# Where the last two column sums of the sample path keep their PSUM banks

## The chip, the cores and the metric

The kernel runs on one core of a Trainium2 chip. Its time is the device time of one execution in microseconds (us). The runs before the change gave 1930.2, 1940.83 and 1928.2 us, with a median of 1930.2 us. Less is better.

## The reference

One layer of a decoder is computed for two groups of tokens that share all weights: a prompt of 1024 rows, and a sample of 8 rows, one new token for each of 8 sequences with 8192 cached positions. All arrays are fp32 with a model width of 1024.

```python
q, k, v, logf, u, z = mixer_inputs(rmsnorm(x, g_mix), w_in, ...)     # 8 heads of 64, and a gating branch
x = x + merge_heads(attention, gating, g_att_out, g_sgu_out, w_o)    # sample: attention over a paged cache
x = x + cross_attend(rmsnorm(x, g_cross), mk, mv, w_cq, w_co)        # 4 heads into 256 memory tokens
h = rmsnorm(x, g_ffn) @ w_up                                         # 1024 -> 2 x 2816
hc = conv_b + sum_i conv_w[i] * shifted(h, i)                        # causal, width 3
x = x + (silu(gate) * val) @ w_down                                  # 2816 -> 1024
y = rmsnorm(x, g_final)
```

Both groups go through all of it, and return `y` together with the new keys, values and convolution rows. The part that matters here is the end: the feed-forward step and the final norm, for the sample's 8 rows and for the second half (512 rows) of the prompt.

## The kernel before

**Two streams.** `prompt()` and `sample()` are generators. The loop at lines 1763 to 1777 draws the prompt's steps and puts steps of the sample between them, at a pace that `PACE` gives. This fixes the order in which the instructions are traced. The order in which each engine then gets them is settled when the program is built: a planner (line 1848) plays the traced program through in a time of its own, gives each tile a buffer, and writes one list for each engine. Each engine works through its list in order; an instruction that waits holds up all that stand behind it on its engine.

**Dense products of the prompt.** Each fp32 product is made of three matmuls on a high and a low part (`gemm3`, lines 242 to 248). `wload` (226) loads a weight tile of 512 KB over SyncE's queue into the ring `wr` (4 buffers, line 223), and `split` makes the high part on ScalarE (209, ring `wh`, 5 buffers) and the low part on VectorE (210, ring `wl`, 4 buffers). In `ffn` (1159) the columns go in four groups of 6, 6, 5 and 5 pairs. A group runs its up products (24 matmuls each, written in the profile as `u,wh` and `u,wl`), evacuated by ScalarE (1192, 1193) and VectorE (1194, 1195, 1197), then its eight down products (15 matmuls each in the last group, `wh,u` and `wl,u`).

**PSUM.** There are eight banks. `BA()` takes from a ring of four, `BB()` from a ring of two (`MB` is 0), and `BK()` (123) hands out in turn two of `BA` and one of `BB`. All dense products take their bank from `BK`. Two more banks, `ms` and `dv`, have one buffer each (129, 132). They serve the decode of the sample and, once that is done, the rest of the sample path.

**The end of the sample path** (`sample_rest`, 1479). Weights come over GpSimd's queue in loads of 1 MB into the ring `kv` (4 buffers). In the up step, each of 22 loads feeds eight products with 256 columns into `dv` (1614); after two loads ScalarE copies the bank (1624) and four small products fold it into `ms` (1629). The activation follows (1634 to 1643). In the down step, each of 11 loads (1648) feeds four products with 512 columns (1653): two into a bank `dv`, two into a bank `ms`, in column groups of 32 partitions that are still to be added up. The profile lists each of these fp32 products as two rows. At the end ScalarE copies each bank to SBUF (1664), one product with a 0/1 matrix adds the four column groups (1666), and VectorE adds the result to the residual (1513). Up to the change this last product takes its bank from `BK()`: the first sum takes one of `bb`, the second one of `ba`. The final norm of the sample and its two stores (1668 to 1674) end this path.

**The end of the prompt path.** After the last down products come the residual add (932), the squares (204), the scale (1242) and the store (1243) of each block of rows.

Of the kernel before, what the change touches and what calls it, by code (L numbers as in the profile page):

```python
# [11 lines left out]
AF = mybir.ActivationFunctionType  # L12
# [66 lines left out]
def build(nc, tc, ctx, a, phases=None):  # L79
# [13 lines left out]
    def nm(s):  # L93
        cnt[0] += 1
        return f"{s}_{cnt[0]}"
# [13 lines left out]
    def KV():  # L109
        return dpool.tile([P, 2048], F32, tag="kv", bufs=NKV, name=nm("kv"))  # L110
# [4 lines left out]
    def BA():  # L115
        return psum.tile([P, 512], F32, tag="ba", bufs=4, name=nm("ba"))

    def BB():
        return psum.tile([P, 512], F32, tag="bb", bufs=2 + MB, name=nm("bb"))
# [3 lines left out]
    def BK():  # L123
        turn_[0] += 1
        return BB() if turn_[0] % BR == BR - 1 else BA()
# [3 lines left out]
    def MS():  # L129
        return BB() if MB else psum.tile([P, 512], F32, tag="ms", bufs=1, name=nm("ms"))  # L130

    def DV():
        return psum.tile([P, 512], F32, tag="dv", bufs=1, name=nm("dv"))

    def D2(n=512, dt=F32):
        return dpool.tile([P, 512], dt, tag="d2", bufs=5, name=nm("d2"))[:, :n]
# [5 lines left out]
    mmul = nc.tensor.matmul  # L142
# [12 lines left out]
    selS = cp[:, C_SELS : C_SELS + 8]  # L155
# [1323 lines left out]
    def sample_rest(xs):  # L1479
# [32 lines left out]
        def add(n, ps):  # L1512
            nc.vector.tensor_tensor(xs[n], ps, xs[n], op=ALU.add)
# [65 lines left out]
        for n in range(2):  # L1579
            ps = MS()  # L1580
# [22 lines left out]
        for f4 in range(11):  # L1603
            ps = DV()
            for q in range(2):
# [6 lines left out]
                for k in range(8):  # L1612
# [5 lines left out]
                        start=(k < 4),  # L1618
                        stop=(k >= 4),
# [3 lines left out]
            t = D2()  # L1623
# [21 lines left out]
        ys = [DV(), MS()]  # L1645
        for f2 in range(0, NF, 2):
            raw = KV().rearrange("p (f d) -> p f d", f=2)
            nc.gpsimd.dma_start(raw, a["w_down"][f2 * P : (f2 + 2) * P, :].rearrange("(f p) d -> p f d", p=P))
            for q in range(2):
                f = f2 + q  # L1650
                j = f % 4
                for n in range(2):
                    mmul(
                        ys[n][32 * j : 32 * j + 32, :],
                        g[:, f * 8 : f * 8 + 32],
                        raw[:, q, n * 512 : (n + 1) * 512],
                        start=(f < 4),
                        stop=(f >= NF - 4),
                        tile_position=(0, 32 * j),
                    )  # L1660
            yield 1
        for n in range(2):
            t = D2()
            nc.scalar.activation(t, ys[n], AF.Copy)
            ps = BK()
            mmul(ps[:8, :], selS, t, start=True, stop=True)
            add(n, ps[:8, :])
        r = rms8(xs)
        for n in range(2):
# [85 lines left out]
    def sample():  # L1755
        yield from decode()
        phase[1] = "rest"
        yield from sample_rest(pair("dec"))
# [111 lines left out]
```

## Time and profile before

| | us |
|---|---|
| runs | 1928.2, 1930.2, 1940.83; median 1930.2 |
| the profiled execution: its own time | 1933.38 |
| its span (first to last record) | 1931.6 |
| TensorE busy (PE) in the span | 1821.0 (94%) |
| VectorE, ScalarE, GpSimd busy | 1403.6, 760.8, 475.3 |
| bytes moved in the span | 517.07 MB |

A row of the timeline gives the start in us, the time to the end of the last instruction merged into it, engine, line, operation, `out<-in` and the count; in brackets stands the idle time of the engine before it and what ended it. PE is the matmul side of TensorE, PEld its weight loads. Ends of matmuls are modelled, so the rate is read from the distance of the starts. A table by windows gives for each stretch the busy time of each engine with its count of instructions, then the granted TensorE clock (1.00 is full) and the share of time in which the DMA engines were busy.

### The profile page before, as it was taken

To read this page: it belongs to the slowest core of one execution; us is meant where nothing else is said; L and a number is where in the kernel's file an instruction comes from. 1 tells how busy PE (TensorE), PEld (TensorE's weight loads), DVE (VectorE), ACT (ScalarE), POOL (GpSimd) and SP (SyncE) were. 2 spreads that over 40 slices of the span, in tenths; PEclk is the share of its full clock that TensorE was granted. 3 is DMA by queue.
4 is the path that set the end of the run, shared out by engine and by line. 5 is a ranking of instruction groups with operands and counts; after the bars stand their busy time and mean duration, and the time that the engine had idled before them with its cause. 6 is when DMAs were issued, how large, how long until landed. Compare 5 with 4: busy or idle time off the path is not lost.

```text
span 1931.6 us, 24224 instructions
## 1 busy us (share of the span) xinstructions
PE 1821.0 (94%) x9255; PEld 1300.7 (67%) x9255; DVE 1403.6 (73%) x1662; ACT 760.8 (39%) x1435; POOL 475.3 (25%) x429
## 2 busy tenths in 40 slices
PE   8999989778898999999999999998999998999798
PEld 5987667555676667777767776675665776667456
DVE  4888668777687786989989899888764459553134
ACT  5332356566632535333333233335353333332122
POOL 1322232322123232223331323343312012101200
PEclk9999999899999999999999999998999998999899
DMA  8877988744496875869787889888769467767841
GB/s 322 288 240 274 332 316 294 255 154 144 158 358 242 317 291 196 304 258 347 283 310 289 312 294 362 322 325 308 282 259 344 163 205 252 290 174 290 332 156 65
DMA packets 156372, 517.07 MB, mean 268 GB/s; under 512 B 20168, under 2 KB 41928, under 8 KB 123488
## 3 DMA queue, kind: packets, MB, share of 16 engines
q0 software_dynamic: 56400, 339.04, 47.1%
q1 hardware_dynamic: 92944, 163.89, 24.4%
q10 hardware_dynamic: 6912, 12.59, 1.7%
q8 instruction: 73, 1.20, 0.2%
q14 instruction: 43, 0.35, 0.1%
HBM read 493.63 MB, written 21.84 MB: 267 GB/s over the span
## 4 chain that ended last, share of the span: by engine, by line
PE 64%; DVE 7%; DMA 4%; ACT 3%; issue 2%; POOL 0%; DVEq 0%; POOLq 0%; ACTq 0%; SPq 0%
PE ba L246 9%; PE ba L247 9%; PE ba L248 9%; PE bb L246 5%; PE bb L247 5%; PE bb L248 5%; PE dv L1371 5%; DMA kv<-cache_k,kidx 2%; DVE kv L1312 1%; DMA kv<-w_down 1%; DVE s L1316 1%; PE ba L973 1%; PE ba L975 1%; PE ba L974 1%; PE dv L1614 1%
## 5 line engine op out<-in xcount | busy, mean ns | idle before, releaser
L209 ACT ACTIVATE wh<-wr 128x1024 fp32r<-128x1024 f32 (+2 forms) x220 | 228.8, 1044 | 474.9 <-PE ba L247 147.1
L210 DVE TENSOR_TENSOR wl<-wr,wh 128x1024 fp32r<-128x1024 f32 (+2 forms) x220 | 262.4, 1200 | 146.0 <-PE ba L248 60.6
L1312 DVE TENSOR_TENSOR kv<-kv,d 128x2048 f32<-128x2048 f32 (+1 forms) x139 | 292.4, 2114 | 33.9 <-DMA kv<-cache_k,kidx 31.9
L1306 POOL DMA_INDIRECT kv<-cache_k,kidx x128 | 179.6, 1403 | 556.0 <-DVE s L1316 251.0
L1316 DVE TENSOR_REDUCE s<-kv 128x32 f32<-128x2048 f32 (+1 forms) x139 | 292.1, 2106 | 0.6
L1365 POOL DMA_INDIRECT kv<-cache_v,kidx x128 | 176.2, 1376 | 419.1 <-PE dv L1371 162.4
L246 PE MATMUL ba<-wh,u 128*128 128x512 f32 (+1 forms) x591 | 224.2, 381 | 0.0
L247 PE MATMUL ba<-wl,u 128*128 128x512 f32 (+1 forms) x591 | 223.8, 379 | 0.0
L248 PE MATMUL ba<-wh,u 128*128 128x512 f32 (+1 forms) x591 | 220.8, 378 | 0.5 <-DVE u L210 0.5
L246 PE MATMUL ba<-u,wh 128*128 128x512 f32 (+2 forms) x528 | 206.7, 392 | 1.3 <-DVE u L213 1.2
L247 PE MATMUL ba<-u,wh 128*128 128x512 f32 (+2 forms) x528 | 207.3, 393 | 0.0
L248 PE MATMUL ba<-u,wl 128*128 128x512 f32 (+2 forms) x528 | 206.3, 391 | 0.0
L1371 PE MATMUL dv<-kv,s 128*32 128x512 f32 x1024 | 135.8, 609 | 4.8 <-DMA kv<-cache_v,kidx 4.8
L246 PE MATMUL bb<-u,wh 128*128 128x512 f32 (+2 forms) x336 | 134.9, 401 | 2.2 <-DVE u L213 2.2
L247 PE MATMUL bb<-u,wh 128*128 128x512 f32 (+2 forms) x336 | 133.3, 397 | 2.5 <-DVE u L213 2.5
L248 PE MATMUL bb<-u,wl 128*128 128x512 f32 (+2 forms) x336 | 132.6, 395 | 0.0
L246 PEld LDWEIGHTS ba<-wh,u 128*128 128x128 f32 x591 | 111.3, 188 | 30.1 <-issue 7.1
L248 PEld LDWEIGHTS ba<-wh,u 128*128 128x128 f32 x591 | 110.8, 188 | 26.7 <-issue 4.6
L247 PEld LDWEIGHTS ba<-wl,u 128*128 128x128 f32 x591 | 111.3, 188 | 22.7 <-issue 2.1
L246 PEld LDWEIGHTS ba<-u,wh 128*128 128x128 f32 x528 | 100.3, 190 | 32.9 <-issue 8.0
L247 PEld LDWEIGHTS ba<-u,wh 128*128 128x128 f32 x528 | 100.5, 190 | 31.9 <-issue 11.3
L248 PEld LDWEIGHTS ba<-u,wl 128*128 128x128 f32 x528 | 100.4, 190 | 28.6 <-issue 8.9
(419 smaller groups left out, 3124.1 us busy)
## 6 DMA issues: line engine op xcount, KB each, us to landing
wr<-w_up SPq DMA_DIRECT2D x88, 512.0 KB
kv<-w_up POOLq DMA_DIRECT2D x22, 1024.0 KB
wr<-w_down SPq DMA_DIRECT2D x40, 512.0 KB
kv<-w_down POOLq DMA_DIRECT2D x11, 1024.0 KB
wr<-w_in SPq DMA_DIRECT2D x16, 512.0 KB
wr<-w_o SPq DMA_DIRECT2D x16, 512.0 KB
wr<-w_cq SPq DMA_DIRECT2D x16, 512.0 KB
wr<-w_co SPq DMA_DIRECT2D x16, 512.0 KB
```

The source lines that it names most:

```text
L209: nc.scalar.activation(h, src, AF.Copy)
L210: nc.vector.tensor_tensor(l, src, h.bitcast(F32), op=ALU.subtract)
L246: mmul(out, sh, mh, start=(i == 0), stop=False)
L247: mmul(out, sh, ml, start=False, stop=False)
L248: mmul(out, sl, mh, start=False, stop=(i == n - 1))
L973: mmul(pss[i], mh[k][:, tb], wh, start=(k == korder[0]), stop=False)
L974: mmul(pss[i], mh[k][:, tb], wl, start=False, stop=False)
L1306: nc.gpsimd.indirect_dma_start(kv, None, a["cache_k"], off(kidx[:, b, ch : ch + 1]))
L1312: nc.vector.tensor_tensor(kvv[:, i : i + m, :], kvv[:, i : i + m, :], qb.unsqueeze(1).broadcast_to((P, m, 512)), op=ALU.mult)
L1316: nc.vector.tensor_reduce(s[:, ch * 4 + i : ch * 4 + i + m, :].rearrange("p k h -> p (k h)"), kvv[:, i : i + m, :].rearrange("p k (h d) -> ...
L1365: nc.gpsimd.indirect_dma_start(kv, None, a["cache_v"], off(kidx[:, b, ch : ch + 1]))
L1371: mmul(dv[32 * j : 32 * j + 32, :], s[:, ch * 4 : ch * 4 + 4, :].rearrange("p k h -> p (k h)"), kvv[:, j, :], start=(ch == 0), stop=(ch == ...
```

## The change

At the end of `sample_rest` the two copies now stand ahead of the two products, and the two products take their banks from `DV()` and `MS()` in place of `BK()`.

```diff
+        ts = [D2(), D2()]
         for n in range(2):
-            t = D2()
-            nc.scalar.activation(t, ys[n], AF.Copy)
-            ps = BK()
-            mmul(ps[:8, :], selS, t, start=True, stop=True)
+            nc.scalar.activation(ts[n], ys[n], AF.Copy)
+        for n in range(2):
+            ps = (DV, MS)[n]()
+            mmul(ps[:8, :], selS, ts[n], start=True, stop=True)
             add(n, ps[:8, :])
```

`ys[0]` holds the one `dv` bank and `ys[1]` the one `ms` bank until its copy has read it. `BK()` counts its calls, so that with two calls fewer each later dense product takes the ring that the product two turns before it would have had; from 15 later products, ten had `ba` and five `bb`, and the pattern of two to one goes on.

## The prediction

> **What bounds the kernel now.** The first view is the page: the span, and the rows of TensorE and of its granted clock over 40 slices of 48.3 us each.
>
> ```profile
> span 1931.6 us, 24224 instructions
> PE   8999989778898999999999999998999998999798
> PEclk9999999899999999999999999998999998999899
> ```
>
> TensorE is busy in nearly every slice, and the slices of the second half that fall below 9 with a lower clock are few. The 38th (1787 to 1835 us) is one. The table by windows is the second view, with cuts set where the dense products of the prompt stop and start again.
>
> ```profile
> core 0: us, PE busy (x) PEld busy (x) DVE busy (x) ACT busy (x) POOL busy (x), PEclk, DMA share, GB/s
> 1700.00:1804.00 104.00, 104.00 (x677) 72.92 (x676) 43.16 (x66) 30.87 (x51) 14.12 (x20) 1.00 0.76 254
> 1804.86:1855.81 50.95, 35.70 (x219) 12.68 (x218) 4.21 (x8) 5.99 (x11) 9.39 (x14) 0.80 0.82 320
> 1855.81:1923.90 68.09, 68.05 (x291) 54.08 (x290) 37.06 (x60) 23.24 (x47) 2.19 (x4) 1.00 0.16 56
> ```
>
> Up to 1804 us TensorE has no gap. Then come 51 us in which it works on the sample alone, with holes and at a clock of 0.80, while VectorE and ScalarE rest. Behind them stand 68 us of dense products with hardly any sample work and an idle DMA (0.16). So two kinds of work that overlapped before run one after the other here. The timeline of TensorE shows the seams:
>
> ```profile
> 1804.67 0.40 PE L248 MATMUL ba<-u,wl 128*128 128x512 f32 x1
> ...
> 1854.86 1.02 PE L1666 MATMUL bb<-d,cp 128*8 128x512 f32 x2 [0.76 <-ACT d L1664]
> 1855.81 0.50 PE L246 MATMUL bb<-u,wh 128*128 128x512 f32 x1
> ...
> 1859.98 1.02 PE L1666 MATMUL ba<-d,cp 128*8 128x512 f32 x2
> 1860.93 0.50 PE L246 MATMUL ba<-u,wh 128*128 128x512 f32 x1
> ```
>
> The first dense matmul after the hole is into `bb`, directly behind the sum in `bb`. The first into `ba` follows directly behind the sum in `ba`. By the code the next two calls of `BK()` after the sums give `ba`, then `bb`: the `ba` product is the earlier one, and yet it starts 5.1 us later, in the middle of the `bb` product. What the two products share with the sums is only the ring. I read this as: a ring gives out its buffers in traced order, so no product traced after a sum gets a bank before that sum has one, and the sum gets it only when the sample's last load has been worked off. The other thing that could hold these products is their weights. VectorE's rows of line 210 for `wl` speak against it (the last before the hole and the next one):
>
> ```profile
> 1805.11 1.23 DVE L210 TENSOR_TENSOR wl<-wr,wh 128x1024 fp32r<-128x1024 f32 x1 [3.36 <-PE ba L248]
> ...
> 1866.75 1.23 DVE L210 TENSOR_TENSOR wl<-wr,wh 128x1024 fp32r<-128x1024 f32 x1 [1.42 <-PE ba L248]
> ```
>
> No split for the up products lies between 1805.11 and 1866.75. From 1855.81 to 1866.75 there is time for some 43 dense matmuls beside the second sum, nearly two products of 24, so the weights of at least two were ready by 1806.3.
>
> **The change part by part.** *Removed:* two draws on the rings. The dense products then no longer stand behind the sample's tail, and TensorE may take them in the hole. The hole runs from the next dense start that was due (a dense matmul every 0.23 us, 68.09 / 291 from the table; 1804.67 + 0.23 = 1804.90) to 1855.81: 50.9 us. In it the sample's own work has to be done all the same, at full clock. Its prices come from the stretches where it lay between dense products:
>
> ```profile
> 1792.59 1.07 PE L1614 MATMUL dv<-kv,xsT 128*32 128x256 f32 x16
> 1793.60 1.06 PE L1629 MATMUL ms<-cp,d 128*128 128x8 f32 x8
> 1794.58 1.07 PE L1614 MATMUL dv<-kv,xsT 128*32 128x256 f32 x16
> 1795.58 0.50 PE L247 MATMUL ba<-u,wh 128*128 128x512 f32 x1
> ...
> 1842.32 1.06 PE L1653 MATMUL dv<-kv,d 128*32 128x512 f32 x4 [0.64 <-DMA kv<-w_down]
> 1843.20 1.03 PE L1653 MATMUL ms<-kv,d 128*32 128x512 f32 x4
> ...
> 1828.64 1.32 PE L1653 MATMUL dv<-kv,d 128*32 128x512 f32 x6
> 1829.99 1.26 PE L1653 MATMUL ms<-kv,d 128*32 128x512 f32 x6
> ```
>
> - Up step: a group of 16 rows takes 1.0 us (1794.58 to 1795.58). The timeline has six such groups after 1804.90, so 6.0 us.
> - Folds: 0.98 us for 8 rows (1793.60 to 1794.58), four of them: 3.9 us.
> - Down step, 11 loads: four rows take 0.88 us (1842.32 to 1843.20), so a load alone takes 1.76. Where two loads lie ready they overlap: from 1828.64 to the last start of the x6 row (1829.99 + 1.26 - 0.60 = 1830.65) 16 rows take about 2.2, or 1.1 for each load. The first four loads were issued before 1821, ahead of the activation, and will lie ready together: 4 x 1.1 = 4.4. The other seven I count alone: 7 x 1.76 = 12.3. Together 16.7, between 11 x 1.0 = 11.0 (the row of line 1568 below) and 11 x 1.76 = 19.4.
> - The first sum: 0.95 (1854.86 to 1855.81). The second costs the same in both.
> - Breaking into a dense run:
>
> ```profile
> 1672.06 1.06 PE L1568 MATMUL dv<-kv,d 128*32 128x512 f32 x8
> 1673.06 0.50 PE L246 MATMUL ba<-u,wh 128*128 128x512 f32 x1
> ...
> 1675.34 1.06 PE L1568 MATMUL dv<-kv,d 128*32 128x512 f32 x8
> ```
>
> The period is 3.28 us: 1.00 for the eight rows, nine dense matmuls at 0.23 (2.08), and 0.20 for the switch. I count 12 visits (four in the up step, the burst of four loads as one, seven single loads): 2.4 us; at most 15, at least 10.
>
> The sum: 50.9 - (6.0 + 3.9 + 16.7 + 0.95 + 2.4) = 50.9 - 29.95 = **21 us gained**. With the dear ends (19.4, 15 visits) it is 17.6, with the cheap ones (11.0, 10 visits) 27.0.
>
> *What hides the sample's waits now.* A load that comes late was paid in full in the hole; now there is dense work to take. Whether the list has it in the right places is the planner's doing. The waits of TensorE from 1364 to 1804 us, the whole stretch in which this path ran between dense products, are five rows, of 9.4 us in all, and none names a DMA; the longest is
>
> ```profile
> PE bb L246 <- DVE t L1197: 7.0, 1, 7.0
> ```
>
> So I take nothing for new waits. The upper bound is what the weight loads cost the down step in the hole, from the waits of 1800 to 1860:
>
> ```profile
> PEld dv L1653 <- DMA kv<-w_down: 13.6, 7, 4.3
> ```
>
> That is 13.6 us if every one of them stayed. DMA has the room: 50.95 us at 320 GB/s and 68.09 at 56 are 20.1 MB. Spread over some 98 us that is 205 GB/s, under the 254 of 1700 to 1804, where TensorE had no gap.
>
> *Added:* the sum now waits until the bank it writes has been copied. It waits for that copy already, as its operand: the quoted 0.76 before line 1666 is a wait on line 1664. Behind it on TensorE's list dense products can stand, which lose at most that 0.76 once. *Moved:* the second copy stands ahead of the first sum in the trace, but in the list the two copies are neighbours already, so nothing. The instruction and DMA counts stay. *Shifted:* the products after the sums change rings by two turns; the mix stays two to one, and from 1855.81 to 1923.90 TensorE was busy 68.05 of 68.09 us, so evacuation had room: nothing, and below 1 us either way.
>
> *The end.* These rows carry it:
>
> ```profile
> 1854.21 0.60 ACT L1664 ACTIVATE d<-dv 128x512 f32<-128x512 f32 x1 [29.43 <-PE ms L1653]
> ...
> 1864.69 0.99 SPq L1674 DMA_DIRECT2D o_ys<-dec  x2
> ...
> 1923.46 0.40 PE L248 MATMUL ba<-wh,u 128*128 128x512 f32 x1
> ```
>
> The last dense row starts at 1923.46 and the span ends 8.1 us later, with the last norm and store of the prompt. This tail keeps its length. What comes late next: the sample's down step was worked off at 1854 and its stores were issued at 1864.69; the dense products would end about 1923.9 - 21 = 1903. The sample's tail may slip by some 35 us before it is the end.
>
> *The clock.* A table of short windows shows it in the hole:
>
> ```profile
> 1815.00:1820.00 5.00, 3.74 (x32) 0.51 1.03 415
> ```
>
> The columns are TensorE's busy time, the clock (0.51), DMA share and GB/s; the dense stretches have 1.00. This is why I priced by rows at full clock. [...]
>
> **The rivals.**
> 1. *The list has the sample's steps too early.* The planner expects a load sooner than it lands, and TensorE stands at a down step with dense products behind it. For it: the loads of the hole did come late. Against: no DMA wait in 440 us of the same pattern. Price: between half and all of the 13.6, so 7 to 14 less gain: 1916 to 1923.
> 2. *The change does not do what it says.* If something other than the ring held the dense products, the hole stays: 1930, within 3 us. Against: the seams at 1855.81 and 1860.93, and the weights that were ready.
> 3. *Slower: the sample's tail becomes the end.* If dense products, once free, run ahead of the sample throughout, all 67 us of them are done by 1804.9 + 67.1 = 1872; the sample's stretch of 50.9 us then follows alone, to 1923; then copies, sums, norm and stores, 10.5 us as from 1854.21 to 1864.69, and about 2 to land: 1936 instead of 1931.6, about 1934 by the median. It decides once the tail slips by more than the 35 us. Against: at 1792.59 and at 1672.06 the sample's steps break into the middle of a dense product, so they go first when ready.
>
> **How the numbers follow.** The profiled execution's own time is 1933.38, 1.8 above its span and 3.2 above the median of the runs. 1933.38 - 21 = 1912.4, and by the median 1930.2 - 21 = 1909. The forecast's own bounds are 1903 (27.0) and 1913 (17.6); I give it 0.73, the first rival 0.15, the second 0.08, the third 0.04. The range goes from 1903 to 1923 and takes in the first rival; outside are the other two, 0.12, and the edges. A measurement of this kernel tells about 1% from no change, which is 19.3 us. Four fifths of the forecast lie beyond it: 0.73 x 0.8 = 0.58, rounded to 0.60 faster by over 1%. The rest of the forecast, the first two rivals and most of the third make 0.37 within 1%, and 0.03 is left for slower by over 1%.
>
> **What would show it.** The profile after should have dense rows (lines 246 to 248) between the rows of line 1653, no stretch of over 5 us without them before the last of the down products, a granted clock of 1.00 from 1800 on, the two sums back to back in `dv` and `ms`, and the last dense row at about 1903. Everything up to about 1804 us should stand as before. DMA waits before line 1653 with dense rows right behind them would show rival 1; an unchanged hole rival 2; a last store on line 1674 rival 3. The prediction fails by size if the down step costs other than 1.1 to 1.76 us for a load between dense rows.

## The result and the profile after

The changed kernel takes 1909.36 us (median of 1904.94, 1906.85, 1911.87 and 1913.18), the kernel before 1930.97 us (median of 1928.2, 1930.2, 1931.75 and 1940.83). By the medians that is 21.6 us less; the ratio on record is 0.9878, with a 95% interval of 0.9854 to 0.9903. The forecast was 1909. The profiled execution took 1913.18 us. In this kernel the sums stand on line 1667 and the sample's stores on line 1675; lines up to 1660 keep their numbers.

First the page of the kernel after: its span, and TensorE and its clock over 40 slices.

```profile
span 1911.4 us, 24216 instructions
...
PE   8999999778898999999999999998999999899998
...
PEclk9999999989998999999999999998999999899999
```

Before, the 38th slice was a 7 with a clock of 8. Now no slice from the 31st on is below 8 in either row. The table by windows, cut at the same places as before but for the last cut, which is near the end of the dense work, shows what took its place.

```profile
core 0: us, PE busy (x) PEld busy (x) DVE busy (x) ACT busy (x) POOL busy (x), PEclk, DMA share, GB/s
1700.00:1804.00 104.00, 104.00 (x662) 73.19 (x661) 44.11 (x68) 31.52 (x52) 13.41 (x19) 1.00 0.73 252
1804.86:1855.81 50.95, 50.95 (x331) 35.89 (x325) 22.78 (x35) 18.78 (x32) 7.84 (x11) 1.00 0.76 276
1855.81:1903.00 47.19, 47.19 (x195) 28.03 (x192) 18.43 (x31) 11.53 (x28) 3.79 (x6) 1.00 0.34 128
```

TensorE is busy in all of the 50.95 us (35.70 before), at full clock (0.80 before), and VectorE and ScalarE work beside it (22.78 and 18.78 us, 4.21 and 5.99 before). DMA, which stood at 0.82 and then at 0.16, is spread (0.76 and 0.34). The timeline of TensorE has the seams:

```profile
1802.70 1.07 PE L1614 MATMUL dv<-kv,xsT 128*32 128x256 f32 x16
1803.70 1.06 PE L1629 MATMUL ms<-cp,d 128*128 128x8 f32 x8
1804.69 1.07 PE L1614 MATMUL dv<-kv,xsT 128*32 128x256 f32 x16
1805.69 0.50 PE L248 MATMUL ba<-u,wl 128*128 128x512 f32 x1
...
1843.95 1.08 PE L1653 MATMUL dv<-kv,d 128*32 128x512 f32 x8
...
1846.55 1.08 PE L1653 MATMUL ms<-kv,d 128*32 128x512 f32 x8
1847.55 0.50 PE L247 MATMUL ba<-u,wh 128*128 128x512 f32 x1
...
1854.75 0.40 PE L248 MATMUL bb<-u,wl 128*128 128x512 f32 x1
1855.08 1.06 PE L1653 MATMUL dv<-kv,d 128*32 128x512 f32 x4
1855.96 1.03 PE L1653 MATMUL ms<-kv,d 128*32 128x512 f32 x4
1856.92 0.50 PE L246 MATMUL bb<-u,wh 128*128 128x512 f32 x1
...
1886.80 1.02 PE L1667 MATMUL dv<-d,cp 128*8 128x512 f32 x2
1887.66 1.02 PE L1667 MATMUL ms<-d,cp 128*8 128x512 f32 x2
...
1903.80 0.40 PE L248 MATMUL ba<-wh,u 128*128 128x512 f32 x1
```

The sample's rows (1614, 1629, 1653) now stand between dense rows (246 to 248); the longest stretch without a dense row is the burst of four loads, 3.6 us from 1843.95. The sums stand back to back in `dv` and `ms`, and the dense work goes on for 16 us behind them.

To measure the gain in one execution I set both at the same step, the second group of an up-step visit just ahead of the hole. In the timeline of before it is this row:

```profile
1802.86 1.07 PE L1614 MATMUL dv<-kv,xsT 128*32 128x256 f32 x16
```

It answers to 1804.69 after, so this execution was 1.83 us later up to there. From that row to the last dense row it is 1923.46 - 1802.86 = 120.60 us before and 1903.80 - 1804.69 = 99.11 after: 21.5 us. From there to the end of the span it is 8.1 and 7.6, so 22.0 in all. Together with the 1.83 this is the 20.2 between the two spans. So 21.5 of the 22.0 us were gained in the window that the prediction named, and the other 0.5 in the tail behind it.

### The profile page after: what moved, and what is told of

It is laid out like the page before. It is cut to its first block, busy times and chain, and to the rows that moved or that the text cites. A ratio compares the mean times of both kernels' runs of the same rounds, so it can differ in the third digit from the quotient of the medians.

```text
span 1911.4 us, 24216 instructions
## 1 busy us (share of the span) xinstructions
PE 1816.1 (95%) x9255; PEld 1296.3 (68%) x9255; DVE 1404.6 (73%) x1662; ACT 761.7 (40%) x1435; POOL 480.6 (25%) x429
## 4 chain that ended last, share of the span: by engine, by line
PE 66%; DVE 8%; ACT 3%; DMA 3%; issue 2%; POOL 0%; SPq 0%; DVEq 0%; POOLq 0%; ACTq 0%
PE ba L247 9%; PE ba L246 9%; PE ba L248 9%; PE bb L246 6%; PE bb L247 5%; PE bb L248 5%; PE dv L1371 5%; DMA kv<-cache_k,kidx 2%; DVE kv L1312 1%; DVE s L1316 1%; PE dv L1614 1%; PE ba L973 1%; PE ba L975 1%; PE ba L974 1%; PE bb L772 1%
## 5 line engine op out<-in xcount | busy, mean ns | idle before, releaser
L1312 DVE TENSOR_TENSOR kv<-kv,d 128x2048 f32<-128x2048 f32 (+1 forms) x139 | 292.3, 2113 | 28.2 <-DMA kv<-cache_k,kidx 26.9
L1365 POOL DMA_INDIRECT kv<-cache_v,kidx x128 | 181.3, 1416 | 424.2 <-PE dv L1371 169.6
L246 PE MATMUL ba<-wh,u 128*128 128x512 f32 (+1 forms) x596 | 226.9, 382 | 0.0
L248 PE MATMUL ba<-wh,u 128*128 128x512 f32 (+1 forms) x596 | 223.4, 380 | 1.0 <-DVE u L210 1.0
L246 PE MATMUL ba<-u,wh 128*128 128x512 f32 (+2 forms) x520 | 203.0, 391 | 1.3 <-DVE u L213 1.2
L247 PE MATMUL ba<-u,wh 128*128 128x512 f32 (+2 forms) x520 | 203.8, 392 | 0.0
L246 PE MATMUL bb<-u,wh 128*128 128x512 f32 (+2 forms) x344 | 138.2, 402 | 1.8 <-DVE u L213 1.8
L247 PE MATMUL bb<-u,wh 128*128 128x512 f32 (+2 forms) x344 | 136.5, 397 | 2.5 <-DVE u L213 2.5
```

The source lines that it names most:

```text
L246: mmul(out, sh, mh, start=(i == 0), stop=False)
L247: mmul(out, sh, ml, start=False, stop=False)
L248: mmul(out, sl, mh, start=False, stop=(i == n - 1))
L1312: nc.vector.tensor_tensor(kvv[:, i : i + m, :], kvv[:, i : i + m, :], qb.unsqueeze(1).broadcast_to((P, m, 512)), op=ALU.mult)
L1365: nc.gpsimd.indirect_dma_start(kv, None, a["cache_v"], off(kidx[:, b, ch : ch + 1]))
```

## The experiments

**The theory.** A ring gives out its banks in traced order. The two sums draw on the rings and can't be given a bank until the sample's last load has been worked off, so every dense product traced behind them waits for that moment. The rivals: the order of copy and sum, the turns of the rings, or merely sharing a ring, whenever it is drawn on.

**One part alone, and the other (`x1_order`, `x2_banks`).** The change has two parts. The first run has only the copies ahead of the sums, the second only the banks:

```diff
 # x1_order: both copies first, as in the change, and then
             ps = BK()
 # x2_banks: copy, sum, copy, sum as before, but
-            ps = BK()
+            ps = (DV, MS)[n]()
```

> Only the order of the change: both copies stand ahead of both sums, and the sums keep their banks from the prompt's rings. If the rings held the dense products back, the hole of 51 us stays and the time is that of before, 1930 within 4. If the reordering of the copies made the gain, it is 1909.

> Only the banks of the change: each copy is followed by its sum as before, but the sums go to dv and ms. If the rings were the cause, the whole gain is here: 1909 within 4, no stretch without dense rows over 5 us. If the order was the cause: 1930.

The order alone gave 1927.56 us beside 1928.86 for before in the same runs, a ratio of 0.9998 (0.9987 to 1.001). Its trace still has the hole: no dense row starts between 1801.08 and 1849.24. That is a hole of 47.9 us, 3.0 shorter than in the trace of before, with the loads coming at 339 GB/s in place of 320; the medians show no gain from it. The banks alone gave 1907.39, a ratio of 0.9883 (0.9865 to 0.9901), and from the common step to the last dense row their trace takes 99.1 us, as after the change. No gain that can be measured is left for the order.

**The turns of the rings (`x5_shift`).** With two draws fewer, later products change rings. This run has the whole change and puts the turns back:

```diff
             add(n, ps[:8, :])
+        turn_[0] += 2
```

> The change, with the turn counter moved on by two, so that all dense products behind the sums take the rings that they took before the change. If the shift of turns is worth nothing, as I counted it: 1909 within 4. If a part of the gain came from another mix of ba and bb at the end: slower than the change by that part, up to 1930.

1906.76 us, ratio 0.9893 (0.9877 to 0.9909), which is the change's own gain. From the common step to the last dense row its trace, too, takes 99.1 us. The shift of turns is worth nothing that can be measured.

**Sharing a ring, or the place in the trace (`x6_late`).** Here the sums draw on the rings as before, but the sample's last step is traced behind all steps of the prompt:

```diff
+        while not done[0]:
+            yield 1
         for n in range(2):
             t = D2()
             nc.scalar.activation(t, ys[n], AF.Copy)
             ps = BK()
```

(`done[0]` is set behind the loop that draws the prompt's steps.)

> The sums keep their banks from the prompt's rings, with everything else of the kernel before, but the sample's last step is traced only when the whole prompt has been traced. If a ring gives out its buffers in traced order, no dense product stands behind the sums any more and the hole is gone, though the banks are still shared: 1909, and up to 5 more because the sums now get a bank only behind the last dense products, and the sample's norm and stores (some 8 us) may end last. If it is the sharing of the banks as such that costs: 1930.

1911.66 us, ratio 0.9909 (0.9892 to 0.9925): 17.2 us less than before, although the banks are shared. The timeline of TensorE ends like this:

```profile
1904.37 0.40 PE L248 MATMUL ba<-wh,u 128*128 128x512 f32 x1
1904.70 1.03 PE L1668 MATMUL bb<-d,cp 128*8 128x512 f32 x2
1905.56 1.02 PE L1668 MATMUL ba<-d,cp 128*8 128x512 f32 x2
```

And the stores in SyncE's queue:

```profile
1900.11 10.32 SPq L1243 DMA_DIRECT2D o_y<-u  x5
1911.79 0.96 SPq L1676 DMA_DIRECT2D o_ys<-dec  x2
```

The hole is gone, and dense work ends at 1904.37, about as after the change (1903.80). The sums are held until then, and so the sample's stores are now the last thing, 3.0 us ahead of the end of the span (1914.8). This is the third rival of the prediction in a mild form: the sample's tail as the end, for some 3 to 4 us. So it isn't the sharing that made the hole; it is that the sums stood ahead of dense products in the traced order.

**Half the change (`x3_ba`, `x4_bb`).** The first sum has its own bank, the second one still draws on one of the rings. By the theory, products of the other ring run on and those of this ring stop:

```diff
-            ps = (DV, MS)[n]()
+            ps = (DV, BA)[n]()      # x3_ba; (DV, BB) in x4_bb
```

> The change, but the second sum takes a bank of the ba ring; the first one goes to dv. If each ring gives out its buffers in traced order, only the products that take a ba bank are held. The seven up products behind the sums take bb, ba, ba, bb, ba, ba, bb. The first and the fourth can run; the seventh can't, because its low part finds no buffer in wl while the second and third keep theirs. So 48 dense matmuls, 11 us, move into the hole: 1919 within 4. If one sum in either ring holds back all dense products: 1930. If what counts is that one ring is free: 1909.

> The change, but the second sum takes a bank of the bb ring; the first one goes to dv. By traced order in each ring the products in bb are held (first, fourth, seventh), and those in ba can run: second, third, fifth and sixth, 96 dense matmuls or 22 us, about all that the hole has room for, with their results left in the four ba banks. So near the change: 1910 within 5. If one sum in either ring holds back all dense products: 1930.

`x3_ba` took 1925.3 us beside 1932.72 for before, ratio 0.9968 (0.9956 to 0.9981), and `x4_bb` 1922.0, ratio 0.9941 (0.9924 to 0.9958). Both counts of products that ran ahead came true, two whole ones in `bb` and four in `ba`, and both times came out too high. The timeline of TensorE in `x3_ba`:

```profile
1799.58 1.07 PE L1614 MATMUL dv<-kv,xsT 128*32 128x256 f32 x16
...
1822.25 0.50 PE L246 MATMUL bb<-u,wh 128*128 128x512 f32 x1
1822.58 0.40 PE L247 MATMUL bb<-u,wh 128*128 128x512 f32 x1
...
1855.71 1.02 PE L1667 MATMUL dv<-d,cp 128*8 128x512 f32 x2 [0.75 <-ACT d L1664]
1856.57 1.02 PE L1667 MATMUL ba<-d,cp 128*8 128x512 f32 x2
1857.52 0.50 PE L246 MATMUL ba<-u,wh 128*128 128x512 f32 x1
```

The `bb` products stop at 1822.58, and the next dense row, into `ba`, starts directly behind the sum in `ba`. The two rows at 1822.25 and 1822.58 belong to the third `bb` product: they need only the high part of its weights, and it stops ahead of line 248, where it needs the low part, for which the expectation had found no buffer in `wl`. Measured from the row at 1799.58 (1802.86 before), the first sum starts 56.13 us later, and 52.00 before: it slipped by 4.1 us. With these two, 50 dense matmuls, 50 x 0.23 = 11.5 us of dense work, were moved ahead; less the slip that is 7.4, and 7.4 was measured. In `x4_bb`:

```profile
1805.51 1.07 PE L1614 MATMUL dv<-kv,xsT 128*32 128x256 f32 x16
...
1840.00 0.40 PE L248 MATMUL ba<-u,wl 128*128 128x512 f32 x1
...
1870.28 1.02 PE L1667 MATMUL dv<-d,cp 128*8 128x512 f32 x2 [0.75 <-ACT d L1664]
1871.14 1.02 PE L1667 MATMUL bb<-d,cp 128*8 128x512 f32 x2
1872.10 0.50 PE L246 MATMUL bb<-u,wh 128*128 128x512 f32 x1
```

Four products, 96 x 0.23 = 22.1 us, ran ahead and were used up at 1840.00. The rest of the sample's tail then lay bare for 30 us; the sum starts 64.77 us after the row at 1805.51, a slip of 12.8. 22.1 - 12.8 = 9.3, and 10.7 was measured by the medians. In the traces, from the common step to the last dense row (1912.44 and 1916.37), the two gains are 7.7 and 9.7. My expectations had counted only the dense work moved ahead. As long as products stand behind the sums, each microsecond by which that work delays the sums is lost again. In the change no dense product waits for the sums, and the slip is free as long as the sample's tail has room.

**The length of the hole (`x7_before_nodown`, `x8_after_nodown`, `x9_before_nodown_paced`).** The last test takes nine of the eleven loads of the down step away, with their products, from both kernels (the sample's output is then incomplete):

```diff
-        for f2 in range(0, NF, 2):
+        for f2 in range(0, 4, 2):
```

> The kernel before without 9 of the 11 loads of the sample's down step and their products (the sample's output leaves these terms out). In the hole the down step lasts as long as its loads and products: from 1825 to 1854 it would shrink to 3.4 us. So the time falls by about 25: 1906 within 4. If the hole were set by something other than the sample's tail: 1930.

> The changed kernel without the same 9 of 11 loads of the sample's down step (the sample's output leaves these terms out). If the down step costs nothing but its time on TensorE between dense products, the time falls by 2 loads of a burst at 0.86 and 7 single ones at 1.94 (1.84 and the switch, from the timeline of the change): 15 us, to 1894 within 4. If its loads still set the end, it falls by more, up to the 25 of the kernel before.

After the change this gave 1896.11 us, 36.6 below the 1932.72 of before, of which the change is 21.6: nine loads are worth about 15.0 us. By the rows of after, two loads of the burst and seven single ones, each with its switch, are 2 x 0.86 + 7 x 2.04 = 16.0 (my expectation had 1.94 for a single one). In the traces the stretch from the common step to the last dense row takes 99.11 us after the change and 83.05 here (1805.15 to 1888.20), 16.1 less. So the down step costs between dense products what its rows say.

Without the change it gave 1917.01, ratio 0.9924 (0.9908 to 0.9941), where I had expected 1906. The timeline of TensorE shows why:

```profile
1763.29 0.40 PE L247 MATMUL bb<-u,wh 128*128 128x512 f32 x1
...
1810.67 1.88 PE L1666 MATMUL ba<-d,cp 128*8 128x512 f32 x4 [0.77 <-ACT d L1664]
1812.48 0.50 PE L246 MATMUL ba<-wh,u 128*128 128x512 f32 x1
...
1821.61 0.39 PE L248 MATMUL bb<-u,wl 128*128 128x512 f32 x1
```

The dense products stop at 1763.29, more than 40 us earlier than before, in the middle of the sample's up step. Each load is also a step in the loop that mixes the two streams. With nine steps fewer the sums are traced earlier, ahead of more dense products, and the hole begins earlier and is 49 us long all the same. With nine loads gone from both kernels, the change is still worth 1917.01 - 1896.11 = 20.9 us.

These rows show one thing more. The turns fall otherwise here, and both sums draw on `ba` (the row of four). Even so the first `bb` product stops behind its first two matmuls and goes on with line 248 only at 1821.61. By the code its low part needs a buffer of `wl`, and the held `ba` products keep that ring's four (three for a down product, one for an up product); no run takes this apart. Held work can so hold a ring on which no sum draws, as with the third `bb` product of `x3_ba`.

If the reading of the steps holds, keeping nine empty steps must bring the start of the hole back:

```diff
-        for f2 in range(0, NF, 2):
+        for f2 in range(0, 4, 2):
             ...
             yield 1
+        for _ in range(9):
+            yield 1
```

> The kernel before without nine of the eleven loads of the down step, as in the run on the kernel before that left out the same nine, but the nine steps of the two streams' loop that belonged to these loads are kept, empty, so that the two sums are traced between the same dense products as in the kernel before. The sample's output is incomplete. Theory (a product waits for the sums if it is traced behind them, so the place in the traced order sets where the block begins, and the sample's tail sets where it ends): dense products stop at about 1805 us as before, not at 1763, and start again once two loads, copy and first sum are done, at about 1831; 25 us below the kernel before, 1905 +- 4 by its median of 1930. Rival (the place in the trace is not what begins the block; with the loads gone the planner itself puts the products off): dense products stop at about 1763 again, and the time is that of the run without these steps, 1917.

1905.78 us, ratio 0.9873 (0.9833 to 0.9914). The timeline of TensorE:

```profile
1800.56 0.40 PE L248 MATMUL ba<-u,wl 128*128 128x512 f32 x1
...
1802.88 1.07 PE L1614 MATMUL dv<-kv,xsT 128*32 128x256 f32 x16
1804.96 1.07 PE L1614 MATMUL dv<-kv,xsT 128*32 128x256 f32 x16 [1.01 <-DMA kv<-w_up]
...
1807.85 1.07 PE L1614 MATMUL dv<-kv,xsT 128*32 128x256 f32 x16 [0.83 <-DMA kv<-w_up]
1809.64 1.88 PE L1629 MATMUL ms<-cp,d 128*128 128x8 f32 x8 [0.72 <-ACT d L1624]
...
1825.37 1.88 PE L1668 MATMUL bb<-d,cp 128*8 128x512 f32 x2 [0.76 <-ACT d L1666]
1827.18 0.80 PE L246 MATMUL bb<-u,wh 128*128 128x512 f32 x1
1827.77 0.63 PE L247 MATMUL bb<-u,wh 128*128 128x512 f32 x1
...
1829.90 0.39 PE L246 MATMUL bb<-u,wh 128*128 128x512 f32 x1
```

The last dense row ahead of the hole starts at 1800.56 and the next behind the first sum, at 1827.18: the hole begins where it began before (four dense matmuls behind the same group of the up step), not at 1763, and at 26.4 us it is shorter by the missing loads. Where the sums are traced sets the hole's beginning, and when the sample's tail is done sets its end.

## Why the prediction was right

- **What bounds the kernel: right.** The products were held by the rings' traced order. `x2_banks` shows that the banks are the cause, `x6_late` that it is the order of draws and not the sharing, `x3_ba`, `x4_bb` and `x9_before_nodown_paced` that hole and sums go together.
- **The hole of 50.9 us and what still has to run in it: right, with two terms off that cancel.** I read each price as in the prediction, from the first row of a visit to the next dense start, with the switch (0.20) apart. A group of the up step still takes 1.00 us (1804.69 to 1805.69) and a fold 0.99 (1803.70 to 1804.69), or 0.81 for the last one, which stands alone. There are 12 visits, as counted. Four loads side by side were put at 4.4 us and took 3.6 (1843.95 to 1847.55). A load alone was put at 1.76 and took 1.84 (1855.08 to 1856.92), so seven are 12.9. The first sum was 0.86 and not 0.95. The corrected sum is 6.0 + 3.8 + 3.6 + 12.9 + 0.86 + 2.4 = 29.6, and 50.9 - 29.6 = 21.3; from the common step to the last dense row the trace gives 21.5. Both kinds of load lie outside the 1.1 to 1.76 us that the prediction named as its sign (0.90 and 1.84); only the average of the eleven, 1.50, lies inside. That the two errors cancel is luck, and so is a median within 0.4 us of the forecast, where the runs of the changed kernel lie 8.2 us apart.
- **No new waits: right.** From 1800 us to the end the table of waits has no row for the matmul side of TensorE, and no row that names a DMA. The first rival (steps listed before their loads land) did not come about.
- **The added wait of the sums: nothing, as put.** The copies were done long ahead of the sums. ScalarE's rows:

```profile
1881.63 0.60 ACT L1664 ACTIVATE d<-dv 128x512 f32<-128x512 f32 x1 [10.83 <-PE ms L1653]
1882.13 0.59 ACT L1664 ACTIVATE d<-ms 128x512 f32<-128x512 f32 x1
```

The sums start only at 1886.80, behind dense products that the list had put ahead of them. That order costs the sums 4 us and TensorE nothing.
- **The end: right, with more room than I gave it.** SyncE's rows:

```profile
1892.76 0.95 SPq L1675 DMA_DIRECT2D o_ys<-dec  x2
1899.29 9.52 SPq L1243 DMA_DIRECT2D o_y<-u  x5
```

From the common step to the sample's stores it is now 88.07 us, before 61.83: they slipped by 26.2. With the 3.0 us that `x6_late` shows from those stores to the end of the span, they could be 1911.4 - 3.0 - 1892.76 = 15.6 later still. That makes about 42 us of room where I had put 35. Neither decided anything, but the slip is as large as the gain itself, and `x6_late` shows the room used up.
- **The change does what it says**, so the second rival fell with the hole itself.

The gain of 1.1% by the medians (1.2% by the ratio) is only just beyond the 1%, or 19.3 us, that the prediction put as the least that can be told from no change; by the ratio's interval it is 18.7 to 28.2 us.

## What to carry to other kernels

Where a ring gives out its buffers in traced order, as in this kernel, it holds back everything that is traced behind a late taker, however long ago its buffers came free. So give a late, small consumer a buffer that nothing early shares, or trace it behind the products that must not wait; then check that its own tail still has room before the end. When a stall is only moved in part, subtract the delay that the moved work gives to the event that ends the stall. And where the streams are mixed by counting steps, taking work out also moves everything that is traced after it: keep the steps when you take out the work.

## What the runs showed of the hardware

Two things that the sum had only roughly or not at all. First, column groups side by side: by the code a load uses two of the four column groups. One load alone takes 1.84 us between dense products, with four rows for each bank. In the burst the loads go in pairs, eight rows for each bank, and four of them take 3.6 us, or 0.90 each.

Second, in `x9_before_nodown_paced` the clock fell without a long idle stretch. The table of its short windows has TensorE's busy time, the clock, DMA share and GB/s:

```profile
1804.00:1806.00 2.00, 1.04 (x17) 1.00 0.96 376
1806.00:1808.00 2.00, 1.17 (x15) 1.00 1.02 406
1808.00:1810.00 2.00, 1.28 (x18) 0.85 1.03 398
1810.00:1812.00 2.00, 2.00 (x16) 0.50 1.03 422
```

The longest idle time since the dense work stopped is 1.01 us (the brackets in the timeline above: 1.01, 0.83, 0.72). Still the clock is at half (0.50) by 1810, after some 5 us in which TensorE was a little over half busy (3.49 of the 6.00 us from 1804). It comes back at 1829.90, after 4.5 us without a gap from 1825.37: it is 0.53 from 1828 to 1830 and 1.00 from 1830 to 1834. Until then dense matmuls started about 0.43 us apart, and with six of them at 0.43 in place of 0.23 this return cost the dense work some 1.2 us. What made the clock fall, and what brought it back, no run here takes apart.
